# Two x tiles and the last mixed tile turned on TensorE by an identity, and a planner with other durations

## The chip, the cores and the metric

The kernel runs on one core of a Trainium2 chip. TensorE (PE) multiplies, VectorE (DVE), ScalarE (ACT) and GpSimd (POOL) work on tiles, and SyncE (SP) issues every DMA, the transposing ones too. The metric is the device time of one execution in microseconds (us). Three runs of the kernel before gave 849.52 us as their median (849.27 to 850.23).

## The reference

One layer of an encoder is computed for a prompt of 512 tokens and for a sample of 1024 tokens, with width 1024. Cut to what matters:

```python
h = rmsnorm(x, g_norm)
qa, ka, va, ga, qb, kb, vb, gb = split(h @ w_in)             # 512,128,128,512,512,512,512,512
oa = attention(axial_rope(rms(qa)), axial_rope(rms(ka)), va) * silu(ga)     # 8 heads of 64, 2 kv heads
a1, a2 = softmax(rope(q1) @ rope(k1).T), softmax(rope(q2) @ rope(k2).T)
ob = rmsnorm((a1 - lam * a2) @ vb) * (1 - lam_init) * silu(gb)              # 4 heads of 128
y = rmsnorm(x + concat(oa, ob) @ w_out, g_final)
```

## The kernel before

The 1536 tokens are 12 tiles of 128 rows: tiles 0 to 3 are the prompt, 4 to 11 the sample. Every fp32 operand of a matmul is split into a high and a low fp16 part, and a product is three matmuls (high by high, high by low, low by high). A weight block is squared (L318, L314), its scale found, and then split eight times over, by ACT into `wh` (L363) and by DVE into `wl` (L367). Each x tile is squared on ACT (L544), scaled into the high half of `xs` on ACT (L393), its low half made on DVE (L396), and the 128x2048 fp16 tile is turned by one transposing DMA (`x_turn`, L423) into `xT`, which holds 16 blocks of 128x128 and is the stationary operand of the projections (L470 to L472). Tile 0 has its square and its high half cut in two, one for ACT and one for DVE.

The program has four stages on PE. First the blocks `kva` (keys and values of group A, 256 columns) and `qa` (512 columns) are projected for all 12 tiles. Then the 80 units of attention of group A run: a unit is 4 score matmuls (`S`, L1093), a maximum on DVE, an exponential on ACT, a split, a transposing DMA into `pT`, and 24 value matmuls (`oa`). Then come the 48 units of group B (16 for the prompt, 32 for the sample), each with 4 or 8 score matmuls (L1204, L1241) and 12 or 24 value matmuls (`ob`, L1283 to L1285). In between stand "fillers": the projections `ga`, `vb`, `kb`, `qb`, `gb` and the output products `po` (L1421 to L1423), so that PE has work while a unit's exponential and transpose are under way. A tile's output product follows its gate: the values are squared, a root is taken, the gate is multiplied in (`mixed`, L1323), the row is normed (L1329, L251), split into `ms` (L1389 on ACT, L1337 on DVE), and turned by a DMA into `mT` (L1341). The last tile's output product is cut in three, 512, 256 and 256 columns, and then scaled and written.

The order on each engine is fixed by a planner in the kernel. Every piece of work is an `op(engine, duration, function, deps, uses)`; the planner runs a list schedule with these written durations, gives the engine whatever is ready and is due first, and emits the instructions in the order of the planned starts. A wrong duration costs nothing in itself, but it sets another order, and each engine then works strictly in that order. PE's due times (`want`) come from a sequence built by hand: each unit of group A lets `RATE_A` fillers in, a unit of group B `RATE_P` (prompt) or `RATE_S` (sample). `margin` makes a load due earlier by that many us. PSUM tiles rotate: 2 for scores (`S`), 2 for values (`O`), 2 for products (`F`).

```python
        debt += rate
        while debt >= 1 and rest:
            seq.append(rest.pop(0))
            debt -= 1
```

Of the kernel before, what the change touches and what calls it, by code (L numbers as in the profile page):

```python
# [34 lines left out]
RATE_A = 5.1  # L35
RATE_P = 4.0
RATE_S = 4.6
# [180 lines left out]
def kernel(ctx, tc, x_prompt, x_sample, g_norm, w_in, a_q_norm, a_k_norm,  # L218
# [23 lines left out]
    ident = const.tile([P, P], F32, name="ident")  # L242
# [245 lines left out]


    first, warm_ps, warm_b = [], [], buf("F")  # L490
    x_buf = [None] * NT
    x_in = [None] * NT
    def plan_x(t, xr_b=None):
# [3 lines left out]
        if t < 2:  # L497
            first.append(f)
        if t == 0:
# [28 lines left out]
            lo = op("DVE", 1.28, lambda: x_low(t), [h1, h2], [xr_b, xs_b])  # L528
            x_in[t] = op("SP", 1.6, lambda: x_turn(t), [lo], [xs_b, x_buf[t]], kb=512, turn=True, land=2.2)
# [22 lines left out]
        a = op("ACT", 1.24, square, [f], [xr_b, xs_b])  # L552
# [10 lines left out]
    def plan_ropes():  # L563
# [55 lines left out]
    def plan_w(nm, b, gate=()):  # L619
# [36 lines left out]
        d = op("POOL", 0.55, lambda: rsqrt_(cell("s_" + nm), box["t1"]), [c])  # L656
# [132 lines left out]
    def post_kva(t, last, b):  # L789
# [35 lines left out]
    def post_rows(t, nm, last, b):  # L825
# [8 lines left out]
        if nm == "qa":  # L834
# [13 lines left out]
        ro = op("DVE", 1.45, lambda: rope_mult(pv(), 8, rope_t[c][:, tt, :], rope_t[s_][:, tt, :], nsub, box),  # L848
# [153 lines left out]
    lc = op("ACT", 1.7, lambda_2, [lb])  # L1002
# [53 lines left out]
    def plan_turn(st, dep, p_b, low_on):  # L1056
# [17 lines left out]
        d_low = {("DVE", True): 1.3, ("DVE", False): 0.73, ("POOL", True): 2.15, ("POOL", False): 1.16}  # L1074
# [6 lines left out]
    def plan_a(ts, hs):  # L1081
# [46 lines left out]
        m = op("DVE", 1.4 if n == 1 else 1.55, peak, [s, qsc_in[t]], [s_b])  # L1128
        e = op("ACT", 1.33 if n == 1 else 1.85, exp, [m], [s_b, p_b])
# [6 lines left out]
    def plan_gate_a(ts, exps_, last):  # L1136
# [15 lines left out]
        a = op("DVE", 0.4, factor, exps_ + [w_ops["ga"][0]])  # L1152
# [22 lines left out]
    def plan_loads(g):  # L1175
        for i in range(2):
# [3 lines left out]
            kb_in[g, i].margin = 12.0  # L1180
# [7 lines left out]
    def plan_b(ts, h):  # L1188
# [7 lines left out]
        if T == 512:  # L1196
# [29 lines left out]
            for i in range(2):  # L1226
                n = op("ACT", 0.93, lambda i=i: exp(i), [n], [s_b, p_bs[i]])
# [63 lines left out]
    def plan_gate_b(ts, es, last):  # L1291
# [62 lines left out]
        e = op("POOL", 0.5, floor, es + [w_ops["vb"][0]])  # L1354
# [15 lines left out]
        def norm_1():  # L1370
            ve.tensor_scalar(ts.mss, ts.mss, 2.0 ** -20, 1e-30, op0=ALU.mult, op1=ALU.max)
# [201 lines left out]
```

## Time and profile before

| | before |
|---|---|
| median of 3 runs | 849.52 us |
| the profiled execution | 847.55 us, its span 845.8 us |
| PE busy | 797.5 us, 94% of the span |
| DVE, ACT, POOL busy | 657.1, 581.4, 370.7 us |
| granted TensorE clock, mean | 0.987 |

A busy time is the sum over an engine's instructions in the span. PE stands idle for 48.3 us of the span; what ended such an idle stretch is named by the view of waits. The granted clock is 1.00 where TensorE runs at its full 2.4 GHz and 0.5 where it runs at 1.2 GHz.

### The profile page before, as it was taken

The page shows a single profiled execution, that of the slowest core. Times are in us where ns is not written, and L with a number is a line of the kernel's source. Part 1 is how long each engine was busy: PE and PEld are TensorE (multiplying, and loading weights), DVE is VectorE, ACT ScalarE, POOL GpSimd, SP SyncE. Part 2 cuts the span into 40 slices and gives each one's busy share as a digit, 9 for nine tenths or more (in the row PEclk, how much of TensorE's full clock was granted, in tenths as well). Part 3 has the DMA queues.
Part 4 walks back from the last instruction along what each step waited for, and adds up shares of the span by engine and source line. Part 5 has one row for each costly group of instructions (what it writes and reads, how often), then busy time and mean ns, then how long its engine had stood idle before and what let it go on. Part 6 is the DMA issues. An engine that isn't in the chain of part 4 may idle for free. (4 is left out here: it accounts for less than half of the span.)

```text
span 845.8 us, 16504 instructions
## 1 busy us (share of the span) xinstructions
PE 797.5 (94%) x6169; PEld 433.7 (51%) x6169; DVE 657.1 (78%) x1062; ACT 581.4 (69%) x1031; POOL 370.7 (44%) x377
## 2 busy tenths in 40 slices
PE   4999989999999999999999989899999999999885
PEld 2566634455555555555555445455555555555443
DVE  6888588687676878798777778677888999988832
ACT  6884259688568895567556866677888878777521
POOL 2689651000000104334253432345677777768830
PEclk9999989999999999999999999999999999999998
DMA  9999857999999999999999999989999988876942
GB/s 264 288 202 198 201 159 178 211 235 233 228 224 256 233 245 190 212 213 220 195 225 206 249 215 211 279 218 241 314 228 209 191 176 213 210 152 158 231 116 66
DMA packets 402448, 179.55 MB, mean 212 GB/s; under 512 B 364480, under 2 KB 365504, under 8 KB 402368
## 3 DMA queue, kind: packets, MB, share of 16 engines
q1 hardware_dynamic: 402368, 178.50, 94.5%
q8 instruction: 48, 0.79, 0.4%
q14 instruction: 32, 0.26, 0.1%
HBM read 62.33 MB, written 30.41 MB: 110 GB/s over the span
## 5 line engine op out<-in xcount | busy, mean ns | idle before, releaser
L1109 ACT ACTIVATE p<-S,nb,qsc 128x1024 f32<-128x1024 f32 (+1 forms) x96 | 101.4, 1058 | 74.1 <-DVE nb L1101 68.1
L1064 ACT CAST p<-p 128x1024 f16<-128x1024 f32 (+1 forms) x128 | 126.5, 989 | 35.5 <-DVE p L1269 22.2
L1098 DVE TENSOR_REDUCE mx<-S 128x1 f32<-128x1024 f32 (+1 forms) x80 | 97.5, 1219 | 31.9 <-PE S L1093 31.4
L1067 POOL TENSOR_TENSOR p<-p,p 128x1024 f16<-128x1024 f32 (+1 forms) x48 | 93.9, 1957 | 64.0 <-ACT p L1064 60.1
L1067 DVE TENSOR_TENSOR p<-p,p 128x1024 f16<-128x1024 f32 x80 | 102.4, 1282 | 23.5 <-ACT p L1064 23.1
L472 PEld LDWEIGHTS <-xT 128*128 128x128 f16 x672 | 66.2, 99 | 72.3 <-issue 3.1
L470 PEld LDWEIGHTS <-xT 128*128 128x128 f16 x672 | 66.7, 99 | 65.2 <-issue 5.6
L471 PEld LDWEIGHTS <-xT 128*128 128x128 f16 x672 | 66.2, 99 | 61.4 <-issue 3.7
L1246 DVE TENSOR_REDUCE mx<-S 128x1 f32<-128x1024 f32 x64 | 77.5, 1217 | 12.8 <-PE S L1241 12.3
L1093 PE MATMUL S<-ka,q 128*128 128x512 f16 x320 | 82.0, 379 | 2.2 <-ACT p L1109 2.1
L1421 PE MATMUL po<-wh_wo,mT 128*128 128x512 f16 (+1 forms) x200 | 75.4, 377 | 6.3 <-DMA mT<-ms 6.3
L771 POOL TENSOR_TENSOR t<-t,t 128x512 f32<-128x512 f32 (+1 forms) x36 | 48.1, 1336 | 72.5 <-DVE t L757 72.1
L1255 ACT ACTIVATE p<-S,nb,c_sc_b 128x1024 f32<-128x1024 f32 x64 | 76.8, 1200 | 2.5
L1422 PE MATMUL po<-wl_wo,mT 128*128 128x512 f16 (+1 forms) x200 | 75.4, 377 | 0.0
L1423 PE MATMUL po<-wh_wo,mT 128*128 128x512 f16 (+1 forms) x200 | 75.3, 376 | 0.0
L784 POOL TENSOR_TENSOR qk<-t,qk 128x512 f16<-128x512 f32 x30 | 37.2, 1243 | 80.4 <-ACT qk L780 79.3
L1241 PE MATMUL S<-kb,q 128*128 128x512 f16 x256 | 65.7, 379 | 5.2 <-ACT p L1255 4.5
L1122 PE MATMUL oa<-va,pT 128*128 128x64 f16 x640 | 64.2, 193 | 4.3 <-DMA pT<-p 4.1
L1149 POOL TENSOR_TENSOR sga<-sga,ca 128x512 f32<-128x512 f32 x12 | 14.4, 1206 | 121.5 <-DVE ca L1146 69.3
L1122 PEld LDWEIGHTS <-pT 128*128 128x128 f16 x640 | 57.5, 98 | 15.6 <-DMA pT<-p 7.2
L1124 PE MATMUL oa<-va,pT 128*128 128x64 f16 x640 | 64.2, 193 | 0.0
L1123 PE MATMUL oa<-va,pT 128*128 128x64 f16 x640 | 64.2, 193 | 0.0
(280 smaller groups left out, 2217.5 us busy)
## 6 DMA issues: line engine op xcount, KB each, us to landing
q<-qd SPq DMA_DIRECT2D x24, 256.0 KB, 3.4
q<-qd SPq DMA_DIRECT2D x48, 128.0 KB, 3.5
gd<-th SPq DMA_DIRECT2D x24, 256.0 KB, 3.4
out_dram<-xres SPq DMA_DIRECT2D x11, 512.0 KB, 3.2
qd<-qk SPq DMA_DIRECT2D x18, 256.0 KB, 3.3
xr<-in_x_sample_dram SPq DMA_DIRECT2D x8, 512.0 KB, 4.9
wst_wo<-in_w_out_dram SPq DMA_DIRECT2D x8, 512.0 KB, 5.5
xres<-in_x_sample_dram SPq DMA_DIRECT2D x8, 512.0 KB, 4.5
```

What stands on the lines that cost most here:

```text
L470: pe.matmul(ps[:, :n], xh[t][:, k, :], wh[:, k, :n], start=(k == 0), stop=False)
L1064: se.copy(st["o"][:, 0:T], st["p"][:, :T])
L1067: (ve if low_on == "DVE" else ge).tensor_tensor(out=st["o"][:, T:2 * T], in0=st["p"][:, :T], in1=st["o"][:, 0:T], op=ALU.subtract)
L1093: pe.matmul(st["S"][:, j, :], q[:, h, :], k_a[g][:, h // 4, :], start=first, stop=not first)
L1098: ve.tensor_reduce(st["mx"], S if n == 2 else S.rearrange("p a b -> p (a b)"), axis=AX.X, op=ALU.max)
L1109: se.activation(st["p"][:, w * j:w * j + w], Sf[:, w * j:w * j + w], AF.Exp, bias=st["nb"][:, j:j + 1], scale=qsc[t][:, h:h + 1], accum_ou ...
L1122: pe.matmul(o, pT[:, c, :], v[:, kv, 0:HD], start=(kt == 0), stop=False)
L1246: ve.tensor_reduce(bx["mx"], bx["S"].rearrange("p a b -> p (a b)"), axis=AX.X, op=ALU.max)
L1255: se.activation(p, bx["S"].rearrange("p a b -> p (a b)"), AF.Exp, bias=bx["nb"], scale=cst["sc_b"], accum_out=ts.rs[:, m:m + 1])
L1421: pe.matmul(ps[:, c], mh, blk.wh[:, k, c], start=(k == 0), stop=False)
L1422: pe.matmul(ps[:, c], mh, blk.wl[:, k, c], start=False, stop=False)
L1423: pe.matmul(ps[:, c], ml, blk.wh[:, k, c], start=False, stop=(k == KT - 1))
```

## The change

The function `plan_pe_turn` is new. It turns the 2048 columns of a tile in four parts of 512: four matmuls whose stationary operand is a block of the tile and whose moving operand is a 128x128 fp16 identity, into a PSUM tile of scores' rotation, and a copy of 128x512 out of PSUM on ACT or DVE. It takes the place of the transposing DMA for x tile 0 (parts 1 and 3 copied by DVE), for x tile 1 and for the last tile's `ms` (part 3 by DVE). Tile 0's low half is made in two halves. The last tile's norm and split are cut in halves too, its first output product runs all high terms before the low ones, and its 16 turns stand among the fillers in front of its output products. The third and fourth chunk of the `qa` weights no longer wait for x tile 0's transpose. Some 25 durations are rewritten, of which two lines stand here, and `RATE_A`, `RATE_S` and the margin of the loads of keys for group B change.

```diff
-RATE_A = 5.1
+RATE_A = 5.0
 RATE_P = 4.0
-RATE_S = 4.6
+RATE_S = 4.8
-    ident = const.tile([P, P], F32, name="ident")
+    ident = const.tile([P, P], F16, name="ident")
+    def plan_pe_turn(src, dst, deps, uses, dst_b, on_dve):
+        parts, turns = [], []
+        for half in range(2):
+            s_b = buf("S")
...
+                def blocks(i=i, j=j, box=box):
+                    if "ps" not in box:
+                        box["ps"] = ps_s.tile([P, 2, 512], F32, name="turn", tag="S")
+                    for k in range(4):
+                        c = 512 * i + P * k
+                        pe.matmul(box["ps"][:, j, P * k:P * k + P], src()[:, c:c + P], ident, start=True, stop=True)
+                def move(i=i, j=j, box=box):
+                    o = dst()[:, 4 * i:4 * i + 4, :]
+                    v = box["ps"][:, j, :].rearrange("p (a b) -> p a b", b=P)
+                    ve.tensor_copy(o, v) if i in on_dve else se.copy(o, v)
...
-            lo = op("DVE", 1.28, lambda: x_low(t), [h1, h2], [xr_b, xs_b])
-            x_in[t] = op("SP", 1.6, lambda: x_turn(t), [lo], [xs_b, x_buf[t]], kb=512, turn=True, land=2.2)
+            l1 = op("DVE", 0.66, lambda: low_half(slice(0, H)), [h1], [xr_b, xs_b])
+            l2 = op("DVE", 0.66, lambda: low_half(slice(H, D)), [h2], [xr_b, xs_b])
+            turn_on_pe([h1, h2], [l1, l2])
...
-        r = op("POOL", 0.85, rstd, [a])
+        r = op("POOL", 1.0, rstd, [a])
+        if t == 1:
+            turn_on_pe([h, h], [lo, lo])
+            return
...
-                        kb=256 if small else 512, after=[x_in[0]] if nm == "qa" and h == 2 else (first if small else chain)[-1:], land=2.6 if nm in ("kva", "qa") else None))
+                        kb=256 if small else 512, after=(first if small else chain)[-1:], land=2.6 if nm in ("kva", "qa") else None))
...
-            kb_in[g, i].margin = 12.0
+            kb_in[g, i].margin = 18.0 if g == 0 else 14.0
...
+            na = op("ACT", 0.72, norm_a, [f], [m_b, x4_b])
+            nb = op("ACT", 0.72, norm_b, [m, na], [m_b, x4_b])
+            n2 = op("POOL", 0.55, norm_3, [op("DVE", 0.32, norm_1, [nb])])
+            h = [op("ACT", 0.62, lambda: high_half(0), [n2], [m_b, x4_b]),
+                 op("DVE", 0.48, lambda: high_half(1), [n2], [m_b, x4_b])]
+            lo = [op("DVE", 0.66, lambda i=i: low_half(i), [h[i]], [m_b, x4_b]) for i in range(2)]
+            x = op("X", 0.001, turned, [h[0]], [mT_b])
+            ts.parts, ts.turns = plan_pe_turn(lambda: ts.ms, lambda: ts.mT, [[x, d] for d in h + lo], [x4_b], [mT_b], (3,))
...
+            if last and hf == 0:
+                for k in range(KT):
+                    ops.append(pe_op(0.432, lambda k=k, f=high_terms: f(k), [ts.parts[k // 4], split[k]] + ops[-1:],
+                                     [b, ts.mT_b, w_b]))
+                for k in range(KT):
+                    ops.append(pe_op(0.216, lambda k=k, f=low_term: f(k), [ts.parts[2 + k // 4]] + ops[-1:],
+                                     [b, ts.mT_b, w_b]))
...
-        s = op("DVE", 0.75, lambda: ve.tensor_scalar(ts.xr, ts.xr, ts.yrs, None, op0=ALU.mult), [g, r], [xr_b])
+        s = op("DVE", 1.3, lambda: ve.tensor_scalar(ts.xr, ts.xr, ts.yrs, None, op0=ALU.mult), [g, r], [xr_b])
...
-        fillers += plan_out(ts)
+        fillers += getattr(ts, "turns", []) + plan_out(ts)
```

This is the DVE queue of the kernel before, from the end of the sums over the `qa` weights to the low parts of those weights (`wl_qa`); `va`, `kst` belong to tile 0's keys and values, `xs` is x tile 2, `wt` and `c_s_qa` are the scale of the block.

```order
L314 SCALAR_TENSOR_TENSOR junkv,wss_qa<-wst_qa_321,gn_104 128x512
L800 TENSOR_TENSOR va<-pj_kva_341,va 128x2x64
L643 TENSOR_REDUCE wt_435<-tot_qa 128x1
L644 TENSOR_SCALAR wt_435<-wt_435 128x1
L396 SCALAR_TENSOR_TENSOR xs<-xr,xrs,xs 128x1024
L338 TENSOR_SCALAR wgs<-gn,c_s_qa 128x8
L348 RECIPROCAL c_r_qa<-c_s_qa 128x1
L350 TENSOR_SCALAR c_eps_qa<-c_s_qa 128x1
L738 TENSOR_REDUCE kst<-sq 128x2
L739 TENSOR_SCALAR kst<-kst,c_eps_kva 128x2
L367 SCALAR_TENSOR_TENSOR wl_qa<-wst_qa_242,wgs,wh_qa 128x512 x2
```

The same place on DVE in the changed kernel, up to the first `wl_qa`.

```order
L396 SCALAR_TENSOR_TENSOR xs<-xr,xrs,xs 128x1024
L367 SCALAR_TENSOR_TENSOR wl_kva<-wst_kva_237,wgs,wh_kva 128x256
L338 TENSOR_SCALAR wgs<-gn,c_s_qa 128x8
L348 RECIPROCAL c_r_qa<-c_s_qa 128x1
L350 TENSOR_SCALAR c_eps_qa<-c_s_qa 128x1
L651 TENSOR_TENSOR rope_sa<-rope_sa,gsw_k 128x512
L367 SCALAR_TENSOR_TENSOR wl_qa<-wst_qa_242,wgs,wh_qa 128x512 x2
```

The last `wl_kva` and the rope table `rope_sa` now stand in front of `wl_qa`; `va` and `kst` have moved behind it. Further up the same queue, behind x tile 0, stand the first copies out of PSUM.

```order
L572 SCALAR_TENSOR_TENSOR xs<-xr,xrs,xs 128x512 x2
L509 CAST xT_281<-turn 128x512 x2
L314 SCALAR_TENSOR_TENSOR junkv,wss_qa<-wst_qa_242,gn_104 128x512
L694 TENSOR_REDUCE wt_325<-tot_kva 128x1
L695 TENSOR_SCALAR wt_325<-wt_325 128x1
```

Before, `wt` of the `kva` block came right behind x tile 0's low half (L396); now two copies and one sum over a `qa` chunk stand between them.

This is the end of the ACT queue of the kernel before, from the last tile's square of the values (`sqb`) on; `junk` rows square the output rows `xres` of tile 10 and then of tile 11.

```order
L1303 ACTIVATE sqb<-ob 128x512
L1329 ACTIVATE ms,mss<-mixed 128x1024
L1389 ACTIVATE ms<-mixed,msc 128x1024
L1481 ACTIVATE junk,yss_10680<-xres 128x1024
L1441 ACTIVATE junk,yss_10796<-xres 128x512
```

The same place in the changed kernel.

```order
L1354 ACTIVATE sqb<-ob 128x512
L1444 ACTIVATE ms,mss_10604<-mixed 128x512
L1586 ACTIVATE junk,yss_10585<-xres 128x1024
L1449 ACTIVATE ms<-mixed,msc 128x512
L509 CAST mT<-turn 128x512 x3
L1586 ACTIVATE junk,yss_10755<-xres 128x1024
L1546 ACTIVATE junk,yss_10821<-xres 128x512
```

The norm's square is half as wide, a square of an earlier output tile has come between, and three copies out of PSUM stand where the transposing DMA was waited for. On PE the last value matmuls (`ob`) are followed by 39 product matmuls of earlier tiles in the kernel before, and by 69 in the changed one; then come the 16 turns, and then in both the last tile's 72.

## Rows read from the trace of the kernel before

**Rows 1.** The page: busy time, share and instructions of each engine.

```profile
PE 797.5 (94%) x6169; PEld 433.7 (51%) x6169; DVE 657.1 (78%) x1062; ACT 581.4 (69%) x1031; POOL 370.7 (44%) x377
```

**Rows 2.** PE's waits by releaser: us in total, times, longest.

```profile
PE po L1421 <- DMA mT<-ms: 6.3, 1, 6.3
PE S L1241 <- ACT p L1255: 4.5, 4, 2.7
PE oa L1122 <- DMA pT<-p: 4.1, 5, 1.8
PE pj_ga L470 <- ACT junk L318: 3.5, 1, 3.5
```

**Rows 3.** Stages: length, busy PE, PEld, DVE, ACT, POOL; PEclk, DMA share, GB/s.

```profile
10.24:25.98 15.74, 10.85 (x54) 5.93 (x53) 12.90 (x48) 11.21 (x26) 4.53 (x9) 0.95 1.02 287
...
28.00:116.00 88.00, 87.91 (x529) 51.42 (x527) 69.81 (x173) 49.41 (x107) 68.37 (x86) 1.00 0.87 196
...
127.00:530.00 403.00, 393.70 (x3440) 207.55 (x3437) 312.79 (x486) 283.17 (x473) 94.99 (x67) 1.00 1.05 220
...
600.00:812.00 212.00, 205.25 (x1525) 116.15 (x1524) 182.21 (x219) 163.52 (x270) 153.37 (x142) 0.99 0.90 204
```

**Rows 4.** More stages, the same columns.

```profile
475.00:540.00 65.00, 58.87 (x497) 30.36 (x496) 48.74 (x72) 44.50 (x81) 21.64 (x15) 1.00 1.10 234
...
780.00:792.00 12.00, 9.26 (x55) 4.51 (x54) 11.70 (x16) 7.53 (x13) 10.40 (x11) 0.87 0.98 218
...
827.00:830.00 3.00, 3.00 (x8) 0.99 (x8) 0.00 (x0) 0.00 (x0) 0.00 (x0) 0.53 0.43 175
```

**Rows 5.** Timeline, PE at the end: start, us, line, out<-in, [idle before <-releaser].

```profile
811.85 0.22 PE L1284 MATMUL ob<-vb,pT 128*128 128x128 f16 x1
811.90 0.22 PE L1285 MATMUL ob<-vb,pT 128*128 128x128 f16 x1
...
819.94 0.38 PE L1422 MATMUL po<-wl_wo,mT 128*128 128x512 f16 x1
820.16 0.38 PE L1423 MATMUL po<-wh_wo,mT 128*128 128x512 f16 x1
826.88 0.61 PE L1421 MATMUL po<-wh_wo,mT 128*128 128x512 f16 x1 [6.35 <-DMA mT<-ms]
827.29 0.63 PE L1422 MATMUL po<-wl_wo,mT 128*128 128x512 f16 x1
```

**Rows 6.** Timeline, the last tile's gate on ACT, DVE and SP's queue.

```profile
812.16 0.60 ACT L1303 ACTIVATE sqb<-ob 128x512 f32<-128x512 f32 x1 [1.30 <-PE ob L1285]
...
817.45 1.06 ACT L1329 ACTIVATE ms<-mixed 128x1024 f16<-128x1024 f32 x1 [4.70 <-DVE mixed L1323]
...
819.44 1.15 ACT L1389 ACTIVATE ms<-mixed,msc 128x1024 f16<-128x1024 f32 x1 [0.84 <-POOL msc L251]
...
821.24 1.28 DVE L1337 SCALAR_TENSOR_TENSOR ms<-mixed,msc,ms 128x1024 f16<-128x1024 f32 x1
...
822.59 1.73 SPq L1341 DMA_TRANSPOSE mT<-ms  x1
...
838.95 0.48 DVE L1433 SCALAR_TENSOR_TENSOR xres<-po,mus,xres 128x256 f32<-128x256 f32 x1 [1.08 <-PE po L1423]
```

**Rows 7.** Timeline, DVE and PE at the start.

```profile
23.60 0.28 PE L470 MATMUL pj_kva<-wh_kva,xT 128*128 128x256 f16 x1 [0.94 <-DMA xT<-xs]
24.66 0.42 PE L472 MATMUL pj_kva<-wh_kva,xT 128*128 128x256 f16 x1
25.98 7.42 DVE L367 SCALAR_TENSOR_TENSOR wl_qa<-wst_qa,wgs,wh_qa 128x512 f16<-128x512 f32 x8 [0.16 <-ACT wh_qa L363]
27.89 0.38 PE L470 MATMUL pj_qa<-wh_qa,xT 128*128 128x512 f16 x1
33.33 0.68 DVE L600 TENSOR_TENSOR rope_sa<-rope_sa,gsw_k 128x512 f32<-128x512 f32 x1
34.73 0.68 DVE L759 TENSOR_TENSOR t<-pj_qa,rope_caq 128x512 f32<-128x512 f32 x1
```

More of the change, by code (lines that the diff above doesn't have):

```diff
@@ L487, in pe_op @@
         return op("PE", dur, fn, deps, uses)
+    def plan_pe_turn(src, dst, deps, uses, dst_b, on_dve):
+        parts, turns = [], []
+        for half in range(2):
+            s_b = buf("S")
+            box = {}
+            for j in range(2):
+                i = 2 * half + j
+                def blocks(i=i, j=j, box=box):
[8 more added lines that the diff above has]
+                    ve.tensor_copy(o, v) if i in on_dve else se.copy(o, v)
+                a = op("PE", 0.24, blocks, deps[i], [s_b] + uses)
+                turns.append(a)
+                parts.append(op("DVE" if i in on_dve else "ACT", 0.69 if i in on_dve else 0.58, move, [a], [s_b] + dst_b))
+        return parts, turns
     first, warm_ps, warm_b = [], [], buf("F")
@@ L1370, in norm_1 @@
         def norm_1():
+            ve.tensor_tensor(out=ts.mss[:, 0:1], in0=ts.mss[:, 0:1], in1=ts.mss[:, 1:2], op=ALU.add)
+            ts.mss = ts.mss[:, 0:1]
             ve.tensor_scalar(ts.mss, ts.mss, 2.0 ** -20, 1e-30, op0=ALU.mult, op1=ALU.max)
@@ L1381, in plan_gate_b, with norm_a @@
         else:
-            r = op("POOL", 2.8, root, [s, e, f, w_ops["gb"][0]], [sg_b])
+            r = op("POOL", 3.1, root, [s, e, f, w_ops["gb"][0]], [sg_b])
         m = op("DVE", 0.69, mix, [r], [ts.o_b, sg_b, m_b])
-        n = op("ACT", 1.24, norm, [m], [m_b, x4_b])
         if end:
-            n2 = op("POOL", 0.55, norm_3, [op("DVE", 0.16, norm_1, [n])])
-        else:
-            n2 = op("POOL", 1.6, norm_2, [n])
+            def norm_a():
+                ts.ms = rp.tile([P, 2 * D], F16, name="ms", tag="x4")
+                ts.mss = tiny.tile([P, 2], F32, name="mss2")
+                se.activation(ts.ms[:, D:D + 512], ts.m[:, 0:512], AF.Square, accum_out=ts.mss[:, 0:1])
@@ new lines, in turned @@
+            def turned():
+                ts.mT = late["ep"].tile([P, 2 * KT, P], F16, name="mT")
+            na = op("ACT", 0.72, norm_a, [f], [m_b, x4_b])
[4 more added lines that the diff above has]
+            lo = [op("DVE", 0.66, lambda i=i: low_half(i), [h[i]], [m_b, x4_b]) for i in range(2)]
@@ L1389, in plan_gate_b @@
+            x = op("X", 0.001, turned, [h[0]], [mT_b])
+            ts.parts, ts.turns = plan_pe_turn(lambda: ts.ms, lambda: ts.mT, [[x, d] for d in h + lo], [x4_b], [mT_b], (3,))
+            ts.m_turned = None
+            u = op("DVE", 0.16, undo, [n2])
+            ts.us_in = op("POOL", 0.8, undo_2, [u, w_ops["wo0"][0], w_ops["wo1"][0]])
+            return
+        n = op("ACT", 1.14, norm, [m], [m_b, x4_b])
+        n2 = op("POOL", 1.6, norm_2, [n])
         h = op("ACT", 1.15, lambda: se.activation(ts.ms[:, 0:D], ts.m, AF.Copy, scale=ts.sc), [n2], [m_b, x4_b])
-        lo = op("DVE", 1.28, low, [h], [m_b, x4_b])
+        lo = op("DVE", 1.75, low, [h], [m_b, x4_b])
@@ L1423, in step, with high_terms, low_term @@
                 pe.matmul(ps[:, c], ml, blk.wh[:, k, c], start=False, stop=(k == KT - 1))
-            ops = []
-            for k in range(KT):
-                ops.append(pe_op(0.648 * n / 512, lambda k=k, f=step: f(k), [ts.m_turned, split[k]] + ops[-1:],
-                                 [b, ts.mT_b, w_b]))
+            def high_terms(k, key=key, blk=blk, c=c):
+                if k == 0:
+                    res[key] = ps_f.tile([P, 512], F32, name="po", tag="F")
+                mh = ts.mT[:, k, :]
+                pe.matmul(res[key][:, c], mh, blk.wh[:, k, c], start=(k == 0), stop=False)
+                pe.matmul(res[key][:, c], mh, blk.wl[:, k, c], start=False, stop=False)
+            def low_term(k, key=key, blk=blk, c=c):
+                pe.matmul(res[key][:, c], ts.mT[:, KT + k, :], blk.wh[:, k, c], start=False, stop=(k == KT - 1))
+            ops = []
+            if last and hf == 0:
[5 more added lines that the diff above has]
+                                     [b, ts.mT_b, w_b]))
+            else:
+                for k in range(KT):
+                    ops.append(pe_op(0.648 * n / 512, lambda k=k, f=step: f(k),
+                                     [ts.m_turned, split[k]] + (ts.parts if last else []) + ops[-1:],
+                                     [b, ts.mT_b, w_b]))
             allops += ops
```

78 lines of the change are left out of this document (52 added, 26 removed).

## The prediction

> **What bounds the kernel now.** I read the page's busy times first. PE works in 797.5 of 845.8 us, the next engine, DVE, in 657.1 [rows 1]: the time is PE's work plus the 48.3 us in which PE stands idle, plus what it loses at the low clock. A change that adds no large work to PE can win only there. So the second view is PE's waits [rows 2]: the largest one that the change touches is the 6.3 us in which the last tile's first product waits for the transposing DMA of `ms`. The third is the busy time by stage [rows 3, 4]: group A with its fillers (127 to 530 us) has PE idle for 403.00 - 393.70 = 9.3 us, with the DMA engines at a share of 1.05; group B (600 to 812 us) for 212.00 - 205.25 = 6.75 us, with DVE busy in 182.21 of 212. The timelines of both ends come last [rows 5 to 7], since the edits lie there.
>
> The sum is made against the profiled execution, 847.55 us (span 845.8 and 1.75 around it); the median of the runs is 849.52, that is 1.97 above it, and I add this at the end.
>
> **The end of the program.** The last value matmul starts at 811.90, PE runs 39 products of earlier tiles behind it until about 820.4, and then stands for 6.35 us until 826.88 [rows 5]. In that time ACT and DVE norm and split the tile (from the square at 812.16 to the end of the low half, 821.24 + 1.28 = 822.5) and the DMA turns it (issued at 822.59, landed 4.3 us later) [rows 6]. After the wait TensorE runs at its low level: matmuls of 512 columns start 0.41 us apart against 0.22 before the wait [rows 5], and the granted clock of 827 to 830 is 0.53 [rows 4], a loss of 3.00 x 0.47 = 1.4 us.
>
> What goes: the DMA's 4.3 us, and with the shorter norm (a 512-wide square, 0.60 as the `sqb` row has it, for 1.06) and the high half shared by ACT and DVE (0.6 for 1.15) about 1 us of the chain. What counts more is the order: 69 products, not 39, now stand behind the last value matmul, 69 x 0.216 = 14.9 us of PE work, and the chain from the square to the last low half took 10.4 us. So the turns find their input ready with some 4 to 5 us to spare, and no wait is left but the one behind them: the first high product needs the first copy (0.6 on ACT), while PE still has 12 more turns. The rest of the copies lie beside eight steps of high products (16 x 0.216 = 3.5 us). The squares of earlier output tiles (1.06 on ACT), which now stand between norm and high half, and the sum of tile 10 on DVE in front of part 3's copy use up some of that spare time, not PE's.
>
> What comes: 16 turns. No row shows one. The nearest is the value matmul of the same 128x128 shape, also with a new stationary block each time, at a pitch of 0.056 us (811.85 to 811.90) [rows 5]: 0.9 us. The far bound is a matmul of 512 columns at the low level, 0.41 each, 6.6 us in all; below nothing it can't be. I take 0.9, for shape and type are the same, and 0.2 for the wait behind them. Gain: 6.35 + 1.4 - 0.9 - 0.2 = 6.6 us. What follows the last product (838.95 to 845.8) is the same in both.
>
> The Trainium skill speaks against this term: "TensorE: Matmul & The Clock Gate", section "Part 4: PE-mode transpose", gives about 275 ns for a 128x128 transpose in a kernel's context, and says that the full clock does not engage for that mode. By its figure the turns would cost an estimated 4.4 us and the end would gain 3.1. These blocks are ordinary matmuls with an identity, not that mode, and no run here shows either.
>
> **The start.** PE waits for x tile 1's transpose until 23.60, runs its `kva` partly at the low level (0.42 for a matmul of 256 columns, against 0.28), and starts `qa` at 27.89 without a wait [rows 7]. From there to 116 us PE is full [rows 3], so the start is worth what the first `qa` product moves. It needs x tile 0, long there, and the first `wl_qa`, which DVE begins at 25.98. Turning on PE takes the DMA waits away, but not this one. DVE is busy for 12.90 of the 15.74 us between x tile 0's low half and that point [rows 3]. The change puts three copies of 0.68 (nearest row: DVE's 128x512 multiplication out of PSUM at 34.73) and the rope table of 0.68 in front of it, and takes 0.8 us of tile 0's keys and values away: 12.90 + 2.04 + 0.68 - 0.8 = 14.8 us. With no wait at all `wl_qa` would begin at 10.24 + 14.8 = 25.06, 0.9 earlier; with the 2.8 us of gaps that the queue has now, at 27.9, 1.9 later. The `qa` chunks load earlier, which closes gaps; but the scale of `kva` comes later (two copies and a sum stand in front of it), and ACT gets six copies of 0.6 in its queue ahead of `wh_qa`. I take 26.7, so the first `qa` product at about 27.5, 0.4 earlier. Against that, PE has gaps in `kva` up to there, and the low level may then fall into `qa`, where nothing hides it; half of such a stretch is 0.7. Sum: 0.3 us lost, between 3.8 gained (25.06, and no low-level stretch) and 4 lost.
>
> **The middle.** The rates take 80 x 0.1 = 8 fillers of 3 x 0.216 = 0.65 us out of group A (5.2 us of PE work) and lay 32 x 0.2 = 6.4 of them into group B's sample units. In B, PE's waits are for exponentials and for `pT` [rows 2]; a low-level stretch follows the longest (granted 0.87 over 12 us, 1.6 us lost) [rows 4]. That makes 6.75 + 1.6 = 8.3 us, and every sample unit now has 0.13 us more PE work to cover its chain, 4.2 in sum. DVE's slow `ms` and `xres` rows are also planned nearer to what they take. I take 40% of the 8.3: 3.3 us gained, between 8.3 gained and 3 lost. In A I take 0.5 lost: less cover, a share of 1.05 on the DMA engines, and the new order deals its waits anew; the bounds are the present 9.3 us gained and the whole 5.2 lost. The 3.5 us wait of the first `ga` product [rows 2] stays: DVE still has the eight low parts of `ga` in front of the rope that frees the product's PSUM tile. The earlier due time of the key loads I put at nothing: in SP's queue the second of them keeps its place behind two transposes.
>
> **The sum.** -6.6 + 0.3 - 3.3 + 0.5 = -9.1: 847.55 - 9.1 = 838.4 for a profiled execution, 840.4 for the median.
>
> **The rivals.**
> 1. The start pays as well. For it: both DMA waits and the late `qa` chunks are gone. Against it: DVE's queue. It gives 3.8 + 0.3 more: 836.3. Chance 0.15.
> 2. The DMA engines set group A's pace. For it: their share of 1.05 there [rows 3]. Against it: PE's waits for `pT` are 4.1 us in 80 units [rows 2], so PE still leads. Then A keeps its 403 us, the 5.2 us taken out become waits, and they are paid again in B: 840.4 + 4.7 = 845.1. Chance 0.17.
> 3. The turns are slow, by a low clock or by what loads the stationary block, at 0.216 to 0.41 each: 2.6 to 5.7 us more, 843 to 846.1. The skill's rule on its transpose mode lies in this rival. Chance 0.08.
> 4. The end does not do what it says: another link (ACT's squares of earlier tiles, or tile 10's sum before the last copy) holds the low products until about when the DMA would have landed. Against it: 4 us to spare. Then 846.5 or so. Chance 0.05.
> 5. Slower than before. With all durations new, the order has stretches where scores or values stand with no filler between them. The place is the change from A to B: 475 to 540 us has PE idle for 65.00 - 58.87 = 6.1 us today [rows 4]. Two more stretches like it cost 12.3 and leave no gain in B: 840.4 + 3.3 + 12.3 = 856. It decides against the change once the middle's waits grow by more than the 6.3 us of both ends. Against it: the written durations come nearer to the rows. Chance 0.10.
>
> My forecast has 0.45.
>
> **The numbers.** 840.4 us. Its own range, with the bounds of turns and start, is 836 to 845. Rivals 1 and 2 lie inside 834 to 847.5; what is left out is most of rival 5 and the far ends. Runs of this kernel differ by 0.96 us in 849.52, so about 0.2% (1.7 us) can be told from no change. Faster than 847.8: the forecast, rivals 1 to 3 and a part of 4, 0.86. Within 0.2%: 0.06. Slower: most of rival 5, 0.08.
>
> **What would show it.** At the end: no wait of PE between the last value matmul and the last product above 0.5 us, turns 0.06 apart, granted clock 1.00 throughout; a turn pitch above 0.2 is rival 3, a wait for a copy is rival 4. At the start: `wl_qa` begins between 25 and 28 us, and the first `qa` product between 26.5 and 28.5. In the middle: group B's idle PE at 3 to 6 us; more than 14 us in group A is rival 2, and a patch of over 6 us around the change from A to B is rival 5. The prediction is wrong at its root if PE's idle time has not shrunk by 8 to 12 us, or if PE's busy time has grown by more than 2.

## The result, and the profile after

The changed kernel takes 842.31 us (median of 4 runs) beside 849.88 for the kernel before: 0.990 times, 95% interval 0.986 to 0.994. A repeat on another chip (below) gave 0.992 (0.989 to 0.994). The forecast was 840.4, a gain of 9.1; the gain is 7.6 by the medians. The profiled execution took 843.05 us, its span is 841.0: 4.8 less than the span before, for the profiled execution of the kernel before lay 2 us under its median.

The page of the changed kernel, the row that answers to [rows 1]:

```profile
PE 797.6 (95%) x6217; PEld 434.8 (52%) x6217; DVE 669.4 (80%) x1070; ACT 585.6 (70%) x1041; POOL 374.8 (45%) x377
```

PE is busy as long as before (799.2 us in a second profile, after_again below), with 48 turns more and a mean granted clock of 0.996 for 0.987. Its idle time is 841.0 - 797.6 = 43.4 us, 4.9 less. PE's waits, the answer to [rows 2] (us in all, times, longest):

```profile
PE oa L1173 <- DMA pT<-p: 9.4, 11, 1.9
PE warm L582 <- ACT xs L566: 9.2, 1, 9.2
PE S L1292 <- ACT p L1306: 5.2, 9, 1.3
...
PE S L1144 <- ACT p L1160: 2.4, 2, 2.1
PE pj_gb L470 <- DVE th L951: 2.2, 1, 2.2
...
PE po L1515 <- ACT mT L509: 0.2, 1, 0.2
PE pj_ga L470 <- DVE t L816: 0.2, 1, 0.2
```

The 6.3 us wait for `mT` has become 0.2, and the first `ga` product's 3.5 has become 0.2 too; the waits for `pT` have grown from 4.1 to 9.4. From 127 to 475 us alone, where group A runs, the kernel before had

```profile
PE oa L1122 <- DMA pT<-p: 2.9, 3, 1.8
PE S L1093 <- ACT p L1109: 0.7, 1, 0.7
```

and the changed kernel

```profile
PE oa L1173 <- DMA pT<-p: 5.4, 6, 1.9
PE S L1144 <- ACT p L1160: 2.4, 2, 2.1
PE tot_gb L690 <- ACT p L1160: 1.4, 1, 1.4
```

The stages of the changed kernel, to be read beside [rows 3, 4]:

```profile
116.00:127.00 11.00, 10.77 (x51) 4.73 (x50) 10.06 (x24) 6.49 (x15) 2.85 (x3) 1.00 0.64 213
127.00:475.00 348.00, 337.67 (x2961) 176.89 (x2960) 267.33 (x411) 241.46 (x401) 75.53 (x55) 1.00 1.03 217
127.00:530.00 403.00, 388.68 (x3421) 203.86 (x3419) 313.29 (x480) 281.27 (x469) 93.19 (x69) 1.00 1.04 218
600.00:812.00 212.00, 206.40 (x1535) 116.83 (x1534) 188.79 (x224) 163.39 (x271) 157.75 (x142) 1.00 0.90 205
475.00:540.00 65.00, 58.72 (x517) 30.81 (x516) 54.85 (x83) 47.11 (x85) 21.43 (x17) 1.00 1.11 248
780.00:792.00 12.00, 11.42 (x85) 6.30 (x83) 11.17 (x14) 11.02 (x21) 8.93 (x6) 1.00 1.08 232
827.00:830.00 3.00, 3.00 (x20) 1.84 (x19) 0.86 (x2) 0.03 (x1) 2.08 (x3) 1.00 0.00 0
```

Two stretches of the kernel before that were not shown, in the same columns:

```profile
116.00:127.00 11.00, 7.52 (x23) 2.70 (x22) 10.93 (x20) 5.69 (x13) 4.83 (x5) 0.69 0.81 245
127.00:475.00 348.00, 343.49 (x3025) 181.84 (x3023) 270.90 (x426) 246.60 (x412) 77.39 (x57) 1.00 1.04 220
```

A stretch's length less PE's busy time is its idle PE. From before to after, from 127 to 475 us: 4.5 to 10.3, that is 5.8 lost. Around the first `ga` product: 3.5 to 0.2, and the granted clock there from 0.69 to 1.00 (51 matmuls in those 11 us, 23 before). Group B (600 to 812): 6.8 to 5.6, and the low clock at 780 to 792 is gone. From 812 to the end: 13.2 to 6.9. Up to 28 us: 13.9 to 13.5.

The end of PE's timeline in the changed kernel (to [rows 5]):

```profile
807.51 0.22 PE L1336 MATMUL ob<-vb,pT 128*128 128x128 f16 x1
...
822.24 0.38 PE L1509 MATMUL po<-wh_wo,mT 128*128 128x512 f16 x1
822.46 1.06 PE L504 MATMUL turn<-ident,ms 128*128 128x128 f16 x16
823.75 0.39 PE L1515 MATMUL po<-wh_wo,mT 128*128 128x512 f16 x1 [0.23 <-ACT mT L509]
823.97 0.38 PE L1516 MATMUL po<-wl_wo,mT 128*128 128x512 f16 x1
```

and the DVE rows at the end of its gate (to [rows 6]):

```profile
814.49 3.44 DVE L1455 SCALAR_TENSOR_TENSOR ms<-mixed,msc,ms 128x512 f16<-128x512 f32 x2
...
834.38 0.48 DVE L1538 SCALAR_TENSOR_TENSOR xres<-po,mus,xres 128x256 f32<-128x256 f32 x1 [1.08 <-PE po L1509]
```

The low halves are done at 817.9, the turns begin at 822.46: 4.5 us to spare, although the two low halves took 3.44 us, beside a GpSimd multiplication of 128x1024. The 16 turns stand 0.056 us apart, and products of 512 columns 0.22 apart behind them.

At the start (to [rows 7]), GpSimd, DVE and PE:

```profile
24.15 1.27 POOL L651 TENSOR_TENSOR rope_saq<-rope_sa,gsw_q 128x512 f32<-128x512 f32 x1 [0.74 <-DVE c_gg L645]
24.25 2.25 DVE L396 SCALAR_TENSOR_TENSOR xs<-xr,xrs,xs 128x1024 f16<-128x1024 f32 x1
25.38 2.24 POOL L651 TENSOR_TENSOR rope_caq<-rope_ca,gain_q 128x512 f32<-128x512 f32 x1
26.43 1.48 DVE L367 SCALAR_TENSOR_TENSOR wl_kva<-wst_kva,wgs,wh_kva 128x256 f16<-128x256 f32 x1
...
28.84 2.74 DVE L367 SCALAR_TENSOR_TENSOR wl_qa<-wst_qa,wgs,wh_qa 128x512 f16<-128x512 f32 x4
28.86 0.38 PE L470 MATMUL pj_qa<-wh_qa,xT 128*128 128x512 f16 x1 [0.19 <-ACT wh_qa L363]
```

`wl_qa` begins at 28.84, not at 26.7, and the first `qa` product at 28.86, 1.0 later than before.

### The profile page after: what moved, and what is told of

It is laid out like the page before. It is cut to its first block, busy times and chain, and to the rows that moved or that the text cites. A ratio compares the mean times of both kernels' runs of the same rounds, so it can differ in the third digit from the quotient of the medians.

```text
span 841.0 us, 16621 instructions
## 1 busy us (share of the span) xinstructions
PE 797.6 (95%) x6217; PEld 434.8 (52%) x6217; DVE 669.4 (80%) x1070; ACT 585.6 (70%) x1041; POOL 374.8 (45%) x377
## 4 chain that ended last, share of the span: by engine, by line
PE 44%; DVE 20%; DMA 12%; POOL 8%; issue 7%; ACT 7%; SPq 1%; POOLq 0%; ACTq 0%; DVEq 0%
DMA pT<-p 6%; PE S L1292 4%; DVE mx L1149 3%; PE po L1507 3%; PE po L1508 3%; PE po L1509 3%; PE S L1144 3%; DVE p L1118 3%; DVE mx L1297 2%; DVE p L1320 2%; PE pj_gb L470 2%; PE pj_gb L471 2%; PE pj_gb L472 2%; DMA wst_kb<-in_w_in_dram 2%; ACT p L1115 2%
## 5 line engine op out<-in xcount | busy, mean ns | idle before, releaser
L1118 DVE TENSOR_TENSOR p<-p,p 128x1024 f16<-128x1024 f32 x80 | 106.8, 1338 | 25.7 <-ACT p L1115 25.2
L1118 POOL TENSOR_TENSOR p<-p,p 128x1024 f16<-128x1024 f32 (+1 forms) x48 | 91.5, 1909 | 68.7 <-ACT p L1115 68.7
L1297 DVE TENSOR_REDUCE mx<-S 128x1 f32<-128x1024 f32 x64 | 77.7, 1217 | 13.0 <-PE S L1292 12.8
L1200 POOL TENSOR_TENSOR sga<-sga,ca 128x512 f32<-128x512 f32 x12 | 13.9, 1156 | 162.4 <-DVE ca L1197 108.7
L1173 PE MATMUL oa<-va,pT 128*128 128x64 f16 x640 | 64.5, 193 | 9.7 <-DMA pT<-p 9.4
L1508 PE MATMUL po<-wl_wo,mT 128*128 128x512 f16 (+1 forms) x192 | 71.1, 370 | 0.0
L1509 PE MATMUL po<-wh_wo,mT 128*128 128x512 f16 (+1 forms) x192 | 71.1, 370 | 0.0
L1507 PE MATMUL po<-wh_wo,mT 128*128 128x512 f16 (+1 forms) x192 | 71.1, 370 | 0.0
L1320 DVE SCALAR_TENSOR_TENSOR p<-p,r,p 128x1024 f32<-128x1024 f32 (+1 forms) x48 | 66.6, 1388 | 1.8
L1175 PE MATMUL oa<-va,pT 128*128 128x64 f16 x640 | 64.4, 193 | 0.0
```

Source lines behind the costliest of these rows:

```text
L1118: (ve if low_on == "DVE" else ge).tensor_tensor(out=st["o"][:, T:2 * T], in0=st["p"][:, :T], in1=st["o"][:, 0:T], op=ALU.subtract)
L1173: pe.matmul(o, pT[:, c, :], v[:, kv, 0:HD], start=(kt == 0), stop=False)
L1297: ve.tensor_reduce(bx["mx"], bx["S"].rearrange("p a b -> p (a b)"), axis=AX.X, op=ALU.max)
L1320: ve.scalar_tensor_tensor(ps[0][:, :T], ps[1][:, :T], ts.r2, ps[0][:, :T], op0=ALU.mult, op1=ALU.add)
L1507: pe.matmul(ps[:, c], mh, blk.wh[:, k, c], start=(k == 0), stop=False)
L1508: pe.matmul(ps[:, c], mh, blk.wl[:, k, c], start=False, stop=False)
```

## The experiments

Twelve kernels ran beside the kernel before, each in 6 or 12 executions; ratios are to it, with 95% intervals. They treat the change as three parts: **end** (the last tile), **start** (x tiles 0 and 1, and the `qa` chunks), **middle** (durations, rates, margins). Idle PE, from the windows of each profile, is given from 127 to 475 us (A), from 600 to 812 (B) and from 812 on. The windows are fixed in time, so a kernel that runs later has another part of its work in them.

| kernel | parts | ratio | A | B | from 812 |
|---|---|---|---|---|---|
| before | none | 1 | 4.5 | 6.8 | 13.2 |
| end_alone | end | 0.9925 (0.9902 to 0.9949) | 6.9 | 7.9 | 7.0 |
| start_alone | start | 0.9972 (0.9953 to 0.9992) | 5.9 | 6.6 | 13.1 |
| middle_alone | middle | 1.0048 (1.0024 to 1.0072) | 10.6 | 8.8 | 9.8 |
| no_middle | start, end | 0.9916 (0.9891 to 0.9940) | 6.1 | 7.5 | 6.9 |
| no_start | end, middle | 1.0019 (0.9999 to 1.0040) | 8.6 | 8.2 | 7.0 |
| no_end | start, middle | 0.9975 (0.9954 to 0.9997) | 10.0 | 6.6 | 8.7 |
| after_again | all | 0.9915 (0.9887 to 0.9943) | 8.3 | 5.8 | 6.9 |
| old_rates | all, old rates | 0.9959 (0.9939 to 0.9979) | 10.1 | 2.8 | 8.5 |
| old_exp | all, two old durations | 0.9958 (0.9939 to 0.9977) | 12.8 | 6.5 | 6.9 |
| late_rope | all, rope tables later | 0.9958 (0.9932 to 0.9985) | 9.3 | 5.6 | 6.9 |
| turns_x6 | all, 80 more turns | 0.9986 (0.9958 to 1.0013) | 14.0 | 6.3 | 6.7 |
| b_only | start, end, B's durations, `RATE_S` | 0.9941 (0.9915 to 0.9968) | 6.5 | 6.0 | 9.9 |

**end_alone.** The kernel before with this of the diff (and the new gate and product order of the last tile):

```diff
-        fillers += plan_out(ts)
+        fillers += getattr(ts, "turns", []) + plan_out(ts)
```

> The kernel before with only the last tile's end changed (norm in halves, 16 turns on PE, high terms first); durations, rates and start are those of before. My theory: the end alone is worth its 6.35 us wait and 1.4 us of low clock less the turns, so 842.3 to 844.0 beside 849.5, no wait of PE above 0.5 us between the last ob and the last product, granted clock 1.00 there, PE idle in 812 to the end down by 6 to 7 us, and the first ga wait of 3.5 us still there. Rival: the gain hangs on the new durations (tile 10's sum, the squares in ACT's queue); then a wait of 2 us or more stands before the first high product and the time is 845.5 or more.

Measured: 6.4 us by the ratio (0.75% of 850.7), and the end as forecast, with 69 products behind the last value matmul. Its waits from 800 us on hold one row:

```profile
PE po L1491 <- ACT mT L509: 0.2, 1, 0.2
```

The wait of the first `ga` product was 0.6, not 3.5, though every engine's order is that of the kernel before up to about 590 us: this wait depends on the execution.

**start_alone.** Of the diff:

```diff
+            turn_on_pe([h1, h2], [l1, l2])
...
+        if t == 1:
+            turn_on_pe([h, h], [lo, lo])
+            return
```

> The kernel before with only x tiles 0 and 1 turned on PE and the qa chunks loaded earlier. My theory: the start loses about 1 us at the first qa product (28.9 against 27.89) because DVE's queue, not the transposes, sets it; 850 to 851 beside 849.5, with the first ga wait 1 us shorter (2.4 for 3.5), which gives the loss back: 849.5 within 0.7. Rival: the start pays, the first qa product stands at 26.5 or earlier, and the time is 847 or less.

Measured: the first `qa` product at 29.30, 0.4 later than expected, and the `ga` wait kept 3.6 us where 2.4 was expected; yet the runs are 0.28% faster. The profiled execution, at 850.87 us among the longest of its runs, doesn't show where from. That stays open. GpSimd's two rope tables and the DVE rows beside them:

```profile
22.80 1.26 POOL L651 TENSOR_TENSOR rope_saq<-rope_sa,gsw_q 128x512 f32<-128x512 f32 x1 [1.04 <-DVE c_gg L645]
22.89 1.46 DVE L367 SCALAR_TENSOR_TENSOR wl_kva<-wst_kva,wgs,wh_kva 128x256 f16<-128x256 f32 x1
...
27.20 1.26 POOL L651 TENSOR_TENSOR rope_caq<-rope_ca,gain_q 128x512 f32<-128x512 f32 x1
27.26 1.23 DVE L338 TENSOR_SCALAR wgs<-gn,c_s_qa 128x8 f32<-128x8 f32 x1 [0.44 <-POOL c_s_qa L251]
```

**middle_alone.** The other lines of the diff: durations, `RATE_A`, `RATE_S`, margins.

```diff
-        a = op("DVE", 0.9, squares, [gains_in])
-        b = op("POOL", 1.65, roots, [a])
-        c = op("DVE", 1.9, scaled, [b])
+        a = op("DVE", 1.2, squares, [gains_in])
+        b = op("POOL", 1.3, roots, [a])
+        c = op("DVE", 1.4, scaled, [b])
...
```

> The kernel before with only the new durations, the two new rates and the margin of the key loads; no turns on PE. My theory: the first ga wait of 3.5 us shrinks by about 2 us, since DVE reaches the low parts of ga 2 us earlier; group A (127 to 475 us) gains 5 to 6 us of idle PE; group B loses 1 to 3. Sum 848.5 to 851.5. Rival: the waits of group A come only with the shifted start, and this kernel then is 845 to 847 with group A's idle PE at 4 to 6 us between 127 and 475.

Measured: 0.48% slower, more than expected, with all of A's new waits and no gain in B. The wait for `mT` fell to 2.0 us without a turn on PE: 60 products, not 39, now stand behind the last value matmul, and 21 x 0.216 = 4.5 us is about what it lost. Its start is worse as well, as in no_start below.

**old_rates.** The changed kernel with

```diff
-RATE_A = 5.0
+RATE_A = 5.1
-RATE_S = 4.8
+RATE_S = 4.6
```

> The changed kernel with RATE_A 5.1 and RATE_S 4.6 as before. If the DMA engines or the missing fillers make group A's new waits (10.3 us of idle PE between 127 and 475, against 4.5 before), the 8 fillers put back cover them: idle 4.5 to 6 there, group B's idle PE up by 1 to 3, total 839 to 841. If the waits come from the order that the new durations give, group A's idle PE stays at 9 to 11 us and the total at 842 to 844.5.

Measured: A keeps its waits, so it is not the fillers taken out of A that make them. Group B's sample units, with fewer fillers (493 product matmuls from their first score matmul to the last value matmul, 508 in the changed kernel, 517 before), have less idle PE, 2.8 us. But the time, 0.9959, is some 3.7 us above after_again (with some 3 of doubt), more than was expected, and part of it stands ahead of those units, which begin at 599.7 us here and at 589.5 in the changed kernel. From 475 to 600 us, the changed kernel and this one:

```profile
475.00:600.00 125.00, 118.72 (x920) 63.14 (x919) 97.70 (x153) 94.30 (x185) 52.60 (x60) 1.00 1.04 244
475.00:600.00 125.00, 114.94 (x868) 59.76 (x867) 91.85 (x144) 88.56 (x174) 47.40 (x52) 0.96 1.02 227
```

Here PE is idle for 10.1 us, for 6.3 in the changed kernel. So the sample units' waits do not follow the number of their fillers, and what the two rates are worth in all is not settled by the window of B.

**after_again.** The changed kernel, unchanged.

> The changed kernel once more, beside the kernel before on the same chip, for a second profile. If group A's idle PE (10.3 us between 127 and 475) belongs to the order, it is there again within 1.5 us, and the ratio stays at 0.990 +- 0.003; if it belongs to one execution, it lies nearer to the 4.5 us of the kernel before.

Measured: the ratio is there again; A's idle PE is 8.3 us, 2.0 less than in the first profile and so outside the 1.5 that was expected of one order.

**no_middle.** Start and end of the diff, nothing else.

> The kernel before with both turned ends (x tiles 0 and 1, last tile) and with its old durations, rates and margins. My theory: the durations bring group A's new waits (10.1 to 10.6 us of idle PE in each kernel that has them, 4.5 to 6.9 in each that has not), so this one has 4.5 to 7 us there, and it is 1 to 4 us faster than the changed kernel. Rival: the sum is not separable; the changed kernel's middle gains more in group B and at the first ga product than it loses, and this one is 2 us or more slower than the changed kernel.

Measured: the same ratio as the changed kernel, neither 1 to 4 us faster nor 2 slower. A is at 6.1, and what that gains goes in B (7.5 us) and at the first `ga` product (2.7 us). These are the windows from 127 to 475 us of end_alone,

```profile
127.00:475.00 348.00, 341.11 (x3000) 180.21 (x2999) 268.92 (x419) 243.91 (x406) 77.00 (x56) 0.99 1.04 218
```

of no_middle,

```profile
127.00:475.00 348.00, 341.88 (x3016) 181.27 (x3014) 270.45 (x424) 246.51 (x410) 75.05 (x57) 1.00 1.03 218
```

and of old_rates:

```profile
127.00:475.00 348.00, 337.90 (x2977) 179.21 (x2976) 267.83 (x416) 240.78 (x401) 76.88 (x55) 1.00 1.05 217
```

The DMA share is alike in all; what differs is PE's busy time in the same 348 us.

**no_start.** The changed kernel with

```diff
-            turn_on_pe([h1, h2], [l1, l2])
+            x_in[t] = op("SP", 1.6, lambda: x_turn(t), [lo], [xs_b, x_buf[t]], kb=512, turn=True, land=2.2)
...
```

> The changed kernel with x tiles 0 and 1 turned by the DMA and the qa chunks as before. If turning them on PE costs 1 us at the first qa product, this kernel has it at 27.9 and is 0 to 1 us faster than the changed one. If it pays, as the -2.4 us of start_alone would have it, this one is 2 us or more slower than the changed kernel.

Measured: 1.0% slower than the changed kernel, some 9 us: the second case (2 us or more), and far beyond what was priced anywhere. ACT and PE at its start:

```profile
28.32 0.27 ACT L824 CAST va<-pj_kva 128x128 f16<-128x128 f32 x1 [4.55 <-PE pj_kva L472]
28.48 3.17 ACT L363 ACTIVATE wh_qa<-wst_qa,wgs 128x512 f16<-128x512 f32 x5
...
29.25 0.38 PE L470 MATMUL pj_qa<-wh_qa,xT 128*128 128x512 f16 x1 [0.97 <-ACT wh_qa L363]
...
34.08 0.38 PE L471 MATMUL pj_qa<-wl_qa,xT 128*128 128x512 f16 x1 [0.87 <-DVE wl_qa L367]
```

With the new durations and the DMA's turn, ACT's queue has `va` of x tile 1 ahead of `wh_qa` and waits 4.55 us for it; PE then stands 2.5 us in `qa` (28 to 116 us; 0.6 in the changed kernel). These 1.9 us are the part that was traced; most of the 9 us was not. So the turns on PE are worth little beside the old durations and much beside the new ones: start and middle cannot be priced apart.

**old_exp.** The changed kernel with

```diff
-        m = op("DVE", 1.45 if n == 1 else 1.55, peak, [s, qsc_in[t]], [s_b])
-        e = op("ACT", 1.33 if n == 1 else 1.7, exp, [m], [s_b, p_b])
+        m = op("DVE", 1.4 if n == 1 else 1.55, peak, [s, qsc_in[t]], [s_b])
+        e = op("ACT", 1.33 if n == 1 else 1.85, exp, [m], [s_b, p_b])
```

> The changed kernel with the old written durations of group A's maximum and exponential alone (1.40 and 1.85 for 1.45 and 1.70). If the shorter exponential makes the planner set the values too early, group A's idle PE falls from 10.3 to 4.5 to 7 us between 127 and 475 and the total by 2 to 5 us; if it is another of the durations, or the order's luck, the idle time stays at 9 us or more.

Measured: A's waits stay (12.8). It is not these two numbers. The time, 0.9958, is some 3.7 us above after_again (with some 3 of doubt); where that comes from isn't shown.

**no_end.** The changed kernel with the last tile's gate and turn of before (and the norm's old duration for every tile).

> The changed kernel with the last tile turned by the DMA and normed whole, as before; start, durations and rates are the changed ones. If the end's gain is its own (PE idle from 812 to the end was 6.85 to 7.0 us in all four kernels with the new end and the new rates or none of them, 13.1 to 13.2 in the two without both), this kernel is 6 to 7 us slower than the changed one: 848 to 850 where the kernel before has 849.7, with one wait of 5 to 6.5 us for the DMA. If the new rates alone leave enough products behind the last value matmul (middle_alone waited only 2.0 us there), the wait is 2 us and this kernel is 845 or so.

Measured between the two: 5.1 us slower than after_again by the ratios (with some 3 us of doubt). Its one wait near the end:

```profile
826.30 0.39 PE L1472 MATMUL po<-wh_wo,mT 128*128 128x512 f16 x1 [1.99 <-DMA mT<-ms]
```

The new durations alone cover 4.3 us of the DMA's wait, as in middle_alone. PE's order is that of the changed kernel up to 622 us, so its A, 10.0, is a profile of the changed kernel's A as well.

**late_rope.** The changed kernel with

```diff
-        q1 = op("POOL", 1.3, lambda: table("q", "ca"), [f, c])
-        q2 = op("POOL", 1.8, lambda: table("q", "sa"), [f, c])
+        q1 = op("POOL", 1.3, lambda: table("q", "ca"), [f, c, w_ops["qa"][1][0]])
+        q2 = op("POOL", 1.8, lambda: table("q", "sa"), [f, c, w_ops["qa"][1][0]])
```

> The changed kernel with GpSimd's two rope tables behind the first low part of the qa weights. If these two instructions slow DVE (the low half of x tile 2 took 2.25 us beside them, 1.28 without; the last wl_kva 1.48 for 0.48), the first takes 1.28 again, the second 0.48, the first wl_qa begins at 26.0 to 26.8 instead of 28.84 and the first qa product at 26.8 to 27.6: 1.3 to 2 us less at the start, and 840 to 841.5 in all if the middle's waits stay as they are. If something else slows DVE there, the two rows keep their 2.25 and 1.48 and the first qa product stays above 28.3.

Measured, DVE and PE at the start:

```profile
23.86 1.28 DVE L396 SCALAR_TENSOR_TENSOR xs<-xr,xrs,xs 128x1024 f16<-128x1024 f32 x1
25.06 0.48 DVE L367 SCALAR_TENSOR_TENSOR wl_kva<-wst_kva,wgs,wh_kva 128x256 f16<-128x256 f32 x1
...
26.47 6.92 DVE L367 SCALAR_TENSOR_TENSOR wl_qa<-wst_qa,wgs,wh_qa 128x512 f16<-128x512 f32 x8 [0.61 <-ACT wh_qa L363]
27.34 0.38 PE L470 MATMUL pj_qa<-wh_qa,xT 128*128 128x512 f16 x1
```

The start does all that was expected, 1.5 us. The two tables now run beside the first two `wl_qa`, which took 1.27 and 1.75 us, where the others took 0.74. The total did not follow: 0.9958. Its order differs from `qa` on, and the first `ga` product waits 2.5 us again.

**turns_x6.** The changed kernel with, for the last tile alone,

```diff
-                    for k in range(4):
+                    for k in list(range(4)) * (6 if src() is not xs[0] and src() is not xs[1] else 1):
```

> The changed kernel with every turn of the last tile issued six times (80 matmuls more, the order of all engines up to there the same). At the pitch of 0.056 us that the trace shows it is 4.5 us longer than the changed kernel (0.5%); at 0.216 each it would be 17 us longer, at the 0.275 that the Trainium skill gives for a transpose 22. For the middle, with the same order for the third time: idle PE between 127 and 475 us of 8 to 10.5 us if it belongs to the order.

Measured, the turns on PE:

```profile
827.30 5.52 PE L504 MATMUL turn<-ident,ms 128*128 128x128 f16 x96
```

95 steps in 5.52 - 0.22 = 5.3 us: 0.056 each. The time is 0.7% above after_again (6.0 us with some 3 of doubt, 4.5 expected). A's idle PE came to 14.0, above what was expected: with one and the same order up to the turns it was 10.3, 8.3 and 14.0 (and 10.0 in no_end).

**b_only.** no_middle with `RATE_S = 4.8` and the new durations of group B's gate, split, exponential and output row, such as

```diff
-        r = op("POOL", 2.8, root, [s, e, f, w_ops["gb"][0]], [sg_b])
+        r = op("POOL", 3.1, root, [s, e, f, w_ops["gb"][0]], [sg_b])
```

> Both turned ends with the new RATE_S and the new durations of group B's work alone (the split on GpSimd, exponential, floor, root, low half, output row); the durations of everything up to group A, RATE_A and the margins are those of before. PE's order is that of no_middle up to a point behind group A. If the durations of group A's side make its new waits, idle PE between 127 and 475 us is 4.5 to 7 (8.3 to 14.0 in the three profiles of the changed kernel), and if those of group B give B its gain, idle PE from 600 to 812 is 5.5 to 6.5 (7.5 in no_middle, 5.6 to 6.3 in the changed kernel): then 839 to 841, ratio 0.987 to 0.990, faster than both kernels. If it is the execution and not the order that deals the waits, the time stays with no_middle and the changed kernel at 842 to 844, ratio 0.990 to 0.993.

Measured: A 6.5 and B 6.0, both as expected; the time, 845.7 for 839 to 841, is not. Tile 10's product now waits 3.1 us at 813 us for its own DMA turn:

```profile
PE po L1507 <- DMA mT<-ms: 3.1, 1, 3.1
```

No kernel tried beats the changed one beyond the intervals. Three that differ from it by one small edit (old_rates, old_exp, late_rope) came out some 0.4% above after_again, which no expectation had.

## Why the prediction came out, step by step

**The end, -6.6: right.** The span's last part gained 6.3 us of idle PE and 1.4 of low clock against 16 turns of 0.056; end_alone gives 6.4 by itself, and of the changed kernel's gain of 7.6 this is most. The pitch taken from the value matmul [rows 5] was the turns' own, and rival 3 is out. The Trainium skill's price for transpose mode ("TensorE: Matmul & The Clock Gate", "Part 4: PE-mode transpose": about 0.275 us) does not carry over to these ordinary matmuls with an identity, at 0.056. What the prediction missed is that the term is not the turns' alone: the new durations put 60 products behind the last value matmul, and with them the DMA's wait is 2.0 us.

**The start, +0.3: size off.** "I take 26.7" for `wl_qa` failed; it was 28.84, outside the window given. The sum counted DVE's own instructions, at durations they have undisturbed. It left out that the earlier rope loads also bring GpSimd's two tables beside DVE's low parts, which took 2.25 and 1.48 us there and 1.28 and 0.48 with the tables moved (late_rope). That is 2.0 of the 2.1 us. Each table costs DVE about 1.0 us wherever it falls on its work (0.5 where DVE had stood idle beside a part of it, in late_rope). With the old durations it fell elsewhere: in start_alone on a `wl_kva` (1.46 for 0.47) and on the scale `wgs` (1.23 for 0.22), 2.0 us again ahead of a `wl_qa` that began at 29.83; in the kernel before on the last two `wl_qa`, behind the point that counts:

```profile
29.96 3.44 DVE L367 SCALAR_TENSOR_TENSOR wl_qa<-wst_qa,wgs,wh_qa 128x512 f16<-128x512 f32 x2
```

Two undisturbed ones take 1.4. So the price stood in the trace from which the sum was made. The Trainium skill ("GPSIMD Engine Reference", "1. Specifications") says that GpSimd and VectorE contend for their SBUF interfaces where a DVE instruction has two SBUF inputs; both slowed rows of the changed kernel have two, and the trace agrees. Two smaller slips of the sum: ACT gets five copies ahead of `wh_qa`, not six, and the bound of 3.8 us gained has no working, for 25.06 is 0.9 earlier and a low-level stretch is worth 1.4. Rival 1's price hangs on that bound.

**Group A, +0.5: wrong.** It lost 5.8 in this profile. The step was "less cover, and the new order deals its waits anew": the cover was priced, the order was not. Five profiles with the old durations for this stage have 4.5 to 6.9 us of idle PE between 127 and 475, nine with the new ones 8.3 to 14.0, with either start and either end, the nine with either rates too. Up to there PE has only two orders in the five, and five in the nine. b_only shows that it is not B's durations, old_exp that it is not those of maximum and exponential; which of the others it is stays open, and so does the new margin of the key loads, which all nine have, none of the five has, and no run tried alone. Nor is the 5.8 a net loss: taken from 116 to 600 us, with the `ga` product's wait and the passage to group B, idle PE is 13.8 to 16.5 us in the five and 14.5 to 22.0 in the nine, and the two ranges overlap. Rival 2 gave the right size, but its reason is not what the runs show: its sign (more than 14 us of idle PE between 127 and 530) is there, at 14.3, but the DMA share did not rise, the turns of `p` took a median of 5.3 us from issue to landing from 127 to 475 us (5.1 before), waits for `pT` are 2.5 of the 5.8, and the old rates do not bring it back.

**The first `ga` product, "stays": wrong.** It gained 3.3 us of idle PE and some 2.7 of low clock behind it (51 matmuls for 23 are 6.0 us at 0.216). Part of this was never the kernel's: with an unchanged order the wait was 0.6 in end_alone, and it lies between 0 and 2.5 in the nine profiles with the new durations, between 0.6 and 3.6 in the five with the old.

**Group B, -3.3: the sum about right, the reason not borne out.** 1.2 us less idle and some 1.6 of low clock at 789. The reason given was the cover of 6.4 more fillers, that is 19 matmuls, in the sample units. They have 9 fewer than before (508 for 517), since the new end puts 30 behind the last value matmul (no_middle: 487) and the new rate gives back 21. And old_rates, with 493, has the least idle PE there, 2.8 us, though not with the time from 475 us counted in (12.9 us for 11.9).

**The root.** "Idle time shrunk by 8 to 12" failed by the letter: 4.9 in this profile, 7.6 in after_again (span 839.9), 0.3 in turns_x6 with the same order up to the turns. Rival 5's sign, over 6 us of idle PE from 475 to 540, is met too (65.00 - 58.72 = 6.3), but the kernel before has 6.1 there: the sign could not tell. The total came right since the end was right and was most of it; A's loss and the gain at `ga`, neither foreseen, about cancel, and that is luck. One profile of each kernel cannot price such terms: between two executions of one order A's idle PE differs by up to 5.7 us, as much as the terms that were argued about.

## What to carry to other kernels

A wait at the end of a program is a term that can be summed and comes out: the work behind it is fixed and nothing is dealt anew later. In a kernel whose order comes from a list schedule, every edit of a number or a dependency ahead of the middle deals the middle's waits again, by several us of either sign here; price such terms by several profiles of several orders, not by one. When an edit brings a GpSimd instruction beside DVE's splits, count DVE's rows at the duration they have beside GpSimd.

## What was not expected of the hardware

DVE's 128x1024 split of two SBUF tensors took 2.25 us beside a GpSimd multiplication of 128x512 and 1.28 without; of 128x256, 1.48 and 0.48; of 128x512, 1.75 and 0.74. The GpSimd instruction itself took 2.24 there, 1.72 beside `wl_qa` in late_rope and 1.26 in start_alone. Of the two that meet, the one that began first was not slowed, and the other ended a little less than its own time behind it: the 128x1024 split began 0.10 us after a table that took its 1.27, and ended 1.08 after it. A 128x128 block turned by an ordinary fp16 matmul with the identity costs 0.056 us at a granted clock of 1.00, in a run of 96 as in a run of 16. The runs of one kernel, 0.96 us apart in the three given, lie between 844.7 and 854.9 in 34 of 35 runs on another chip: the 0.2% that the prediction took for the limit of what can be told was too fine.
